# 68 dense expert tiles instead of 72 in a hybrid mLSTM, S5 and PEER block: fewer dense tiles, more gather steps, other buffer counts

## The chip, the core and the metric

The kernel runs on one core of a Trainium2 chip. TensorE multiplies matrices, VectorE (DVE in the profile) and ScalarE (ACT) work element by element, GpSimd (POOL) issues indirect DMAs (gathers by a list of row numbers), and SyncE (SP) issues ordinary DMAs. The metric is the device time of one execution in microseconds; it is compared as the median of several runs. The profiles come from single executions.

## The reference

The input is 512 tokens of 2048 features in float32. One layer is computed: a norm, an input projection, an mLSTM mixer beside an S5 state-space mixer, an output projection with a residual sum, and then the PEER part, which is what the change touches:

```
q   = rmsnorm(h) @ wq                        # 8 heads, two halves of 128
s   = q . subkeys                            # 128 scores for each half
idx = top 16 of (top 16 of s1 + top 16 of s2)    # expert number = i1 * 128 + i2
gate = softmax(top scores)
act = gelu(x . u_tab[idx])                   # 128 (token, expert) pairs per token
h  += sum over pairs of gate * act * v_tab[idx]
out = rmsnorm(h) * final_g
```

There are 128 x 128 = 16384 experts, each with a row of 2048 numbers in `u_tab` and one in `v_tab`. Each of the 512 tokens picks 128 experts, so there are 65536 pairs.

## The kernel before

Gathering two rows for each of the 65536 pairs would be slow, so the kernel treats most experts densely. `NT` tiles of 128 experts are multiplied with all 512 tokens, whether a token picked them or not, and a gate matrix that is zero for the pairs not picked removes the rest. `NF` of these tiles are fixed (the first experts by number); `NSEL` more are lists of the experts picked most often, counted at run time by `select`. Pairs whose expert is in no dense tile are rare pairs. They are handled by gather steps: the tokens are sorted by their number of rare pairs and cut into four blocks of 128; for block b there are `SB[b]` steps on the `u` side and as many on the `v` side, and one step gathers one row of 2048 numbers for each of up to 128 tokens. If a token has more rare pairs than its block has steps (a whole block's worth for the later blocks), `flag` is set and `rare_rest` does what is left behind the V pass, one gather after the other.

All matrix products are made of three passes (`mm3`, lines 114 to 117) over operands split in a high and a low part.

The PEER part has these stages:

- **The U pass** (lines 1555 to 1575) goes through `NT` x 4 units, a quarter tile each. `u_load` brings a tile of 128 expert rows into `ur` (from SP for the fixed tiles, by a gather from GpSimd for the others), two tiles ahead. `u_unit` transposes four blocks on TensorE into PSUM (`tu`), and ScalarE copies the high part `uh`; `u_low` makes the low part `ul` on VectorE; `h_unit` multiplies. After the fourth quarter ScalarE takes the GELU into `hg`, and SP stores it (lines 1503 to 1505). `h_step` keeps transposes three units and low parts two units ahead of the products.
- **Beside it** the same loop hands out side work. Each unit adds a budget (2.9 until the lists are ready, then `UBUD`), and each piece of side work gives back its own cost when it yields. First come the end of the routing, `select`, and `flags`. Then (from unit `n0` on) two jobs share the budget: `gbuild`, 64 pieces at 3.45 that build the gate matrix in eight chunks of 64 tokens, and `rare`, gather steps at 2.5 each. `gbuild` has a due time (`GEND`); when it is ahead of it, gather steps run.
- **A chunk of `gbuild`** makes one-hot operands `go` on VectorE, multiplies 24 small matrices per piece on TensorE, and ScalarE copies the result into `Gb`, of which there is one. Then SP stores 4 MB from it into `gt_d` with four DMAs whose pieces are 256 bytes long (line 1456), and `UT["hold"]` keeps `gbuild` from its next piece for some units.
- **The V pass** (lines 1642 to 1662) goes through `NT` tiles twice, once for each half of the 2048 output columns. A unit loads half a tile of `v` (`vr`), the stored activations (`hgl`) and in half 0 the gate tile (`gt`), multiplies the gate in (`v_gate`, and stores the product in `w_d` for half 1), splits both operands and runs 24 matmuls. The gather steps that the U pass has not done are spread evenly over the units, except the last `VEND`.

A gather step is `row_gather` into a `gr` tile (issued on GpSimd) and one VectorE instruction: `mac_u` (line 1343) or `mac_v` (line 1350). `rare` issues gathers ahead: 2 deep in the U pass, 4 deep in the V pass, where `gr_tile` takes its tiles from two pools of two each.

```
        bud += UBUD if n0 is not None else 2.9
...
            gb_next = n0 is None or n >= UT["hold"] and UT["gb_n"] * (GEND - n0) <= (n - n0) * (T // 8)
            c = pump1("a") if gb_next else 0
            c = c or (pump1("g") if n0 is not None else 0)
```

Of the kernel before, what the change touches and what calls it, by code (L numbers as in the profile page):

```python
# [8 lines left out]
F32 = mybir.dt.float32  # L9
F32R = mybir.dt.float32r  # L10
I32 = mybir.dt.int32
U32 = mybir.dt.uint32
BF16 = mybir.dt.bfloat16
AF = mybir.ActivationFunctionType
OP = mybir.AluOpType
# [4 lines left out]
P = 128  # L20
T = 512
D = 2048
# [3 lines left out]
NEG = -1.0e30  # L26
BIGNEG = -3.0e38
MAGIC = 12582912.0
NF = 28
NSEL = 44  # L30
NT = NF + NSEL
JN = P - NF
CLIP = 32
RW = 64
SB = (54, 36, 31, 26)
JUNK = F32
UBUD = 2.8
GEND = 262
VPRE = 276
VEND = 14  # L40


# [5 lines left out]
def hybrid_block(ctx: ExitStack, tc: tile.TileContext, x, norm1_g, w_in, b_gates, conv_w, mnorm_g,  # L48
# [3 lines left out]
    v, s, g, pe, sp = nc.vector, nc.scalar, nc.gpsimd, nc.tensor, nc.sync  # L52
# [3 lines left out]
    def pool(name, bufs, side="left"):  # L56
        return tc.tile_pool(name=name, bufs=bufs, side=side, reuse_waits="tile")
# [37 lines left out]
    with pool(name="tmp", bufs=1, side="right") as tmp:  # L95
# [8 lines left out]
        p = tp_bank([P, 96])  # L104
# [749 lines left out]
    front.close()  # L854

    pk = ctx.enter_context(pool(name="pk", bufs=1, side="right"))
    subT = pk.tile([P, 2, P], F32, name="subT")
    iotaF = pk.tile([P, P], F32, name="iotaF")
    pcol = pk.tile([P, 1], F32, name="pcol")
    jt = pk.tile([P, P, 2], BF16, name="jt")  # L860
# [4 lines left out]
    DT = pk.tile([P, 5, T], BF16, name="DT")  # L865
# [2 lines left out]
    esel2 = pk.tile([P, 2, NSEL], I32, name="esel2")  # L868
    rl = pk.tile([P, TB, 2 * RW + 1], I32, name="rl")
    flag = pk.tile([P, 1], I32, name="flag")  # L870

    xn_d = dram.tile([T, D], F32, name="xn_d")
    gt_d = dram.tile([P * P, T], F32, name="gt_d")
# [43 lines left out]
    with pool(name="n2", bufs=1) as n2:  # L917
# [18 lines left out]
        p = tp_bank([P, 2, P])  # L936
# [6 lines left out]
        v.tensor_copy(jt, iotaF[:, :, None].to_broadcast([P, P, 2]))  # L943
        v.tensor_scalar(tri, iotaF, pcol, None, op0=OP.is_gt)
    mix.close()
    ixs = ExitStack()
    ix = ixs.enter_context(pool(name="ix", bufs=1, side="right"))
    i1T, i2T, gT = (ix.tile([P, T], F32, name=n) for n in ("i1T", "i2T", "gT"))
    tks = ExitStack()
    tk = tks.enter_context(pool(name="tk", bufs=1, side="right"))  # L950
    gate = tk.tile([P, TB, P], F32, name="gate")
# [79 lines left out]
    for h in range(8):  # L1031
# [7 lines left out]
        for a in range(2):  # L1039
            p = tp_bank([P, TB, P])  # L1040
# [7 lines left out]
    UT = {}  # L1048
# [23 lines left out]
    def spread(row, n):  # L1072
        r = row.rearrange("p (a b) -> p a b", b=2)
        return r[:, :, None, :].to_broadcast([P, r.shape[1], n, 2])

    def select():
# [11 lines left out]
        for c2 in range(0, T + 64, 32):  # L1088
            if c2 < T:
                oa = ck.tile([P, 16, JN, 2], BF16, name="oa", bufs=2)  # L1090
                ob = ck.tile([P, 16, P, 2], BF16, name="ob", bufs=2)
                onehot(oa, NF, JN, i1b, c2, 32)
                onehot(ob, 0, P, i2b, c2, 32)
# [7 lines left out]
        c = ck.tile([P, JN], F32, name="c")  # L1101
        v.tensor_scalar(c, cnt, float(CLIP), None, op0=OP.min)
        oha = ck.tile([P, JN, P], BF16, name="oha")
# [9 lines left out]
        p = tp_bank([P, CLIP])  # L1113
# [4 lines left out]
        k = ck.tile([P, 2, CLIP], F32, name="k")  # L1118
# [25 lines left out]
        v.memset(sf, 1.0)  # L1144
        sel = sf[:, NF:]
        v.scalar_tensor_tensor(sel, ex, need, eq, op0=OP.is_lt, op1=OP.mult)
# [9 lines left out]
        ab = ck.tile([P, 2, JN], F32, name="ab")  # L1156
        v.tensor_copy(ab, sli[:, 1:3])
        yield
        ohv = ck.tile([P, JN, 2, NSEL], BF16, name="ohv")
        for j in range(0, JN, 20):  # L1160
            js = slice(j, j + 20)
            v.tensor_tensor(oha[:, js], ab[:, 1, js, None].to_broadcast([P, 20, P]),
                            iotaF[:, None, :].to_broadcast([P, 20, P]), op=OP.is_equal)
            yield
            v.tensor_tensor(ohv[:, js, 1], ab[:, 0, js, None].to_broadcast([P, 20, NSEL]),
                            iotaF[:, None, 1:NSEL + 1].to_broadcast([P, 20, NSEL]), op=OP.is_equal)
            v.tensor_tensor(ohv[:, js, 0], ohv[:, js, 1],
                            iotaF[:, NF + j:NF + j + 20, None].to_broadcast([P, 20, NSEL]), op=OP.mult)
            v.tensor_scalar(ohv[:, js, 1], ohv[:, js, 1], pcol, None, op0=OP.mult)
            yield  # L1170
        p = tp_bank([P, 2, NSEL])
# [151 lines left out]

    def gr_tile():
        UT["n"] = UT.get("n", -1) + 1
        pl = UT["rp2"] if "rp2" in UT and UT["n"] % 4 > 1 else UT["rp"]
        t = pl.tile([P, D], F32, name="gr", bufs=2)
        key = "r2" if "rp2" in UT and pl is UT["rp2"] else "r1"
        UT[key] = UT.get(key, 0) + 1
        if UT[key] <= 2:  # L1330
            v.memset(t, 0.0)
        return t

# [24 lines left out]

    rjobs = [(w, b, j) for w in range(2) for b in range(TB) for j in range(SB[b])]

    def rare():
        q = []
        k = 0
        xa = nx = None
        for n, (w, b, j) in enumerate(rjobs):
            if n == 0 or nx is None and n + 6 < len(rjobs) and rjobs[n + 6][2] == 0 and "rp2" in UT:
                nx = xa_tile()
                gather(nx, h1_d if rjobs[min(n + 6, len(rjobs) - 1)][0] and n else xn_d, tokc(rjobs[n + 6][1] if n else b))
            if j == 0:
                if nx is None:  # L1370
                    nx = xa_tile()
                    gather(nx, h1_d if w else xn_d, tokc(b))
                xa, nx = nx, None
            while k < len(rjobs) and k < n + (4 if "rp2" in UT else 2):
                t = gr_tile()
                row_gather(t, rjobs[k][0], rl[:, rjobs[k][1], rjobs[k][2]:rjobs[k][2] + 1])
                q.append(t)
                k += 1
            t = q.pop(0)
            a = racts[:, b, j:j + 1]  # L1380
            if w:
                mac_v(t, a, xa)
            else:
                mac_u(t, xa, a)
            if j == SB[b] - 1:
                if w:
                    rare_out(b, xa)
                else:
                    rare_w(b, 0, SB[b], racts[:, b, 0:SB[b]])
            UT["rare_n"] = n + 1  # L1390
            yield 2.5
# [31 lines left out]
    def gbuild():  # L1423
        stk = ExitStack()
        gb = stk.enter_context(pool(name="gb", bufs=1, side="right"))
        GC = 64
        GN = 8

        def fill(Gb, o, t0):
            for t4 in range(0, GN, 4):  # L1430
                p = tp_bank([P, 4, P])
                for t in range(4):
                    a, c = divmod(t4 + t, 2)
                    for k in range(3):
                        pe.matmul(p[:, t, :], o[1][:, a, :, c], o[2 + k][:, a, :, c], start=k == 0, stop=k == 2)
                s.activation(Gb[:, :, t0 + t4:t0 + t4 + 4], p.rearrange("p t i -> p i t"), AF.Copy)

        gv = gt_d.rearrange("(i k) t -> k i t", k=P)
        todo = []
        for c in range(0, T, GC):  # L1440
            Gb = gb.tile([P, P, GC], F32, name="Gb")
            for t0 in range(c, c + GC, GN):
                o = [gb.tile([P, GN // 2, P, 2], BF16, name=f"go{i}", bufs=2) for i in range(5)]
                onehot(o[0], 0, P, i1b, t0, GN)
                onehot(o[1], 0, P, i2b, t0, GN)
                for k in range(3):
                    v.tensor_tensor(o[2 + k], o[0], spread(DT[:, 2 + k, t0:t0 + GN], P), op=OP.mult)
                todo.append((Gb, o, t0 - c))
                UT["gb_n"] += 1
                yield 3.45  # L1450
                if len(todo) > 1:
                    fill(*todo.pop(0))
            while todo:
                fill(*todo.pop(0))
            for a in range(0, P, 32):
                sp.dma_start(gv[:, a:a + 32, c:c + GC], Gb[:, a:a + 32, :])
            UT["hold"] = UT["step"] + 4
        stk.close()
        yield 0.1

    ustk = ExitStack()
    up = ustk.enter_context(pool(name="up", bufs=1))

    def u_load(i):
        ur = up.tile([P, D], F32, name="ur", bufs=2)
        if i < NF:
            sp.dma_start(ur, u2[i * P:(i + 1) * P, :])
        else:
            assert UT["sel"]
            gather(ur, u2, esel[:, i - NF:i - NF + 1])  # L1470
        UT["r", i] = ur
# [16 lines left out]

    def u_low(i, q):
        uh, p = UT.pop(("p", i, q))  # L1490
        ul = up.tile([P, 4, P], F32R, name="ul", bufs=4)
        v.tensor_tensor(ul, p, uh.bitcast(F32), op=OP.subtract)  # L1492
        UT["u", i, q] = (uh, ul)

    def h_unit(i, q):
        if q == 0:
            UT["h", i] = mm_bank()
        uh, ul = UT.pop(("u", i, q))
        for a in range(4):
            k = q * 4 + a  # L1500
            mm3(UT["h", i], uh[:, a, :], ul[:, a, :], xh[:, k, :], xl[:, k, :], k == 0, k == 15)
        if q == 3:
            hg = up.tile([P, T], F32, name="hg", bufs=2)
            s.activation(hg, UT.pop(("h", i)), AF.Gelu)
            sp.dma_start(hg_d[i], hg)

# [48 lines left out]
    for n, (i, q) in enumerate(units):  # L1555
# [8 lines left out]
        while bud > 0:  # L1564
# [5 lines left out]
            c = pump1("a") if gb_next else 0  # L1570
            c = c or (pump1("g") if n0 is not None else 0)
# [69 lines left out]
    o = banks()  # L1641
    for n, (h, i) in enumerate(vunits):
        if n == NT:
            for k, b_ in enumerate(o):
                s.activation(F0[:, k // 2, (k % 2) * 512:(k % 2) * 512 + 512], b_, AF.Copy)
            o = banks()
# [21 lines left out]
    with tc.If(fl_v > 0):  # L1668
        rare_rest(fb)
        for tb in range(TB):  # L1670
            t = fb.tile([P, D], F32, name="rg")
# [44 lines left out]
```

## Time and profile before

| | |
|---|---|
| median of 3 runs | 3192.2 us (3181.93 to 3195.36) |
| the profiled execution | 3185.52 us, span 3183.6 us |
| mean granted TensorE clock in it | 0.962 |
| TensorE busy | 2926.7 us, 92% |
| VectorE busy | 2226.3 us, 70% |
| ScalarE busy | 978.8 us, 31% |
| GpSimd busy | 848.9 us, 27% |
| moved by DMA | 691.92 MB, mean 217 GB/s |

The shares are means over stages that differ: the DMA engines are busy for three to four tenths of the first third and almost wholly in the last third. A busy TensorE is not one at its peak, since matmuls overlap and their ends are modelled. The granted clock is given as a share of full speed, 2.4 GHz; its other level is 1.2 GHz.

### The profile page before, as it was taken

To read this page: it belongs to the slowest core of one execution; us is meant where nothing else is said; L and a number is where in the kernel's file an instruction comes from. 1 tells how busy PE (TensorE), PEld (TensorE's weight loads), DVE (VectorE), ACT (ScalarE), POOL (GpSimd) and SP (SyncE) were. 2 spreads that over 40 slices of the span, in tenths; PEclk is the share of its full clock that TensorE was granted. 3 is DMA by queue.
4 is the path that set the end of the run, shared out by engine and by line. 5 is a ranking of instruction groups with operands and counts; after the bars stand their busy time and mean duration, and the time that the engine had idled before them with its cause. 6 is when DMAs were issued, how large, how long until landed. Compare 5 with 4: busy or idle time off the path is not lost. (4 is left out here: it accounts for less than half of the span.)

```text
span 3183.6 us, 44978 instructions
## 1 busy us (share of the span) xinstructions
PE 2926.7 (92%) x17540; PEld 2462.5 (77%) x17540; DVE 2226.3 (70%) x3665; ACT 978.8 (31%) x1491; POOL 848.9 (27%) x656
## 2 busy tenths in 40 slices
PE   7999999999799999998999998896698888899997
PEld 5888978899688887886777787775477666688886
DVE  7467544432388977874767876774688888889885
ACT  5343555432322321121222222221122222232223
POOL 3000111000200000001222222222244888647860
PEclk9999999999899999997999999998899999999999
DMA  4422444353322221634778667779899997999983
GB/s 142 129 87 85 102 108 119 105 175 133 134 87 86 100 95 67 242 140 147 258 241 283 181 193 241 252 245 323 296 395 381 403 401 240 407 408 406 394 328 134
DMA packets 366140, 691.92 MB, mean 217 GB/s; under 512 B 169490, under 2 KB 248850, under 8 KB 320338
## 3 DMA queue, kind: packets, MB, share of 16 engines
q0 software_dynamic: 74240, 393.57, 33.0%
q1 hardware_dynamic: 291680, 295.40, 28.2%
q8 instruction: 140, 2.29, 0.3%
q14 instruction: 80, 0.66, 0.1%
HBM read 644.04 MB, written 96.86 MB: 233 GB/s over the span
## 5 line engine op out<-in xcount | busy, mean ns | idle before, releaser
L115 PE MATMUL mm<-xh,uh 128*128 128x512 f32 x1152 | 494.6, 429 | 0.0
L117 PE MATMUL mm<-xh,ul 128*128 128x512 f32 x1152 | 465.1, 404 | 7.5 <-DVE ul L1492 7.5
L116 PE MATMUL mm<-xl,uh 128*128 128x512 f32 x1152 | 465.3, 404 | 0.0
L1343 DVE SCALAR_TENSOR_TENSOR junk<-gr,xa 128x2048 f32<-128x2048 f32 x147 | 335.8, 2284 | 163.0 <-DMA gr<-in_peer_u_dram,rl 149.0
L1350 DVE SCALAR_TENSOR_TENSOR xa<-gr,racts,xa 128x2048 f32<-128x2048 f32 x147 | 345.4, 2350 | 58.1 <-DMA gr<-in_peer_v_dram,rl 56.8
L112 DVE TENSOR_TENSOR wl<-wr,wh 128x1024 fp32r<-128x1024 f32 (+1 forms) x144 | 187.1, 1302 | 240.2 <-ACT wh L111 240.1
L1484 ACT ACTIVATE uh<-tu 128x512 fp32r<-128x512 f32 x288 | 171.6, 600 | 501.4 <-PE tu L1482 489.4
L1346 POOL DMA_INDIRECT gr<-in_peer_u_dram,rl x147 | 180.2, 1226 | 460.8 <-DVE junk L1343 419.1
L115 PE MATMUL mm<-wh,xh 128*128 128x256 f32 (+1 forms) x1024 | 294.6, 288 | 0.0
L117 PE MATMUL mm<-wh,xl 128*128 128x256 f32 (+1 forms) x1024 | 288.8, 282 | 1.8 <-DVE xl L112 1.8
L116 PE MATMUL mm<-wl,xh 128*128 128x256 f32 (+1 forms) x1024 | 289.0, 282 | 0.0
L116 PE MATMUL tp<-vl,ewh 128*128 128x512 f32 x576 | 232.5, 404 | 61.1 <-DVE vl L112 61.0
L1346 POOL DMA_INDIRECT gr<-in_peer_v_dram,rl x147 | 248.6, 1691 | 131.9 <-DVE xa L1350 83.3
L117 PEld LDWEIGHTS mm<-xh,ul 128*128 128x128 f32 x1152 | 225.7, 196 | 62.4 <-DVE ul L1492 8.7
L117 PE MATMUL mm<-xh,wl 128*128 128x512 f32 x640 | 255.9, 400 | 12.1 <-DVE wl L112 12.1
L111 ACT ACTIVATE ewh<-hgl 128x512 fp32r<-128x512 f32 x144 | 91.0, 632 | 561.4 <-DVE hgl L1546 275.9
L115 PE MATMUL mm<-xh,wh 128*128 128x512 f32 x640 | 258.3, 404 | 0.0
L116 PEld LDWEIGHTS mm<-xl,uh 128*128 128x128 f32 x1152 | 227.5, 197 | 39.6
L115 PEld LDWEIGHTS mm<-xh,uh 128*128 128x128 f32 x1152 | 227.1, 197 | 39.4
L116 PE MATMUL mm<-xl,wh 128*128 128x512 f32 x640 | 254.9, 398 | 0.0
L1482 PE MATMUL tu<-ident,ur 128*128 128x128 f32 x1152 | 182.1, 282 | 73.0 <-DVE ul L1492 72.3
L111 ACT ACTIVATE wh<-wr 128x1024 fp32r<-128x1024 f32 (+1 forms) x144 | 166.8, 1161 | 260.5 <-PE mm L117 103.0
(498 smaller groups left out, 6080.4 us busy)
## 6 DMA issues: line engine op xcount, KB each, us to landing
wr<-in_w_in_dram SPq DMA_DIRECT2D x80, 512.0 KB, 3.6
gt_d<-Gb SPq DMA_DIRECT2D x32, 1024.0 KB, 17.0
ur<-in_peer_u_dram SPq DMA_DIRECT2D x28, 1024.0 KB, 5.0
vr<-in_peer_v_dram SPq DMA_DIRECT2D x56, 512.0 KB, 14.9
hg_d<-hg SPq DMA_DIRECT2D x72, 256.0 KB, 2.2
hgl<-hg_d SPq DMA_DIRECT2D x72, 256.0 KB, 9.3
w_d<-hgl SPq DMA_DIRECT2D x72, 256.0 KB, 7.6
hgl<-w_d SPq DMA_DIRECT2D x72, 256.0 KB, 7.9
```

Source lines behind the costliest of these rows:

```text
L111: s.activation(hi, src, AF.Copy)
L112: v.tensor_tensor(lo, src, hi.bitcast(F32), op=OP.subtract)
L115: pe.matmul(o, ah, bh, start=start, stop=False)
L116: pe.matmul(o, ah, bl, start=False, stop=False)
L117: pe.matmul(o, al, bh, start=False, stop=stop)
L1343: v.scalar_tensor_tensor(UT["junk"], t, 1.0, xg, op0=OP.mult, op1=OP.mult, accum_out=a)
L1346: g.indirect_dma_start(out=t, out_offset=None, in_=v2 if w else u2, in_offset=IOA(ap=col, axis=0), bounds_check=P * P - 1, oob_is_err=False)
L1350: v.scalar_tensor_tensor(acc, t, a, acc, op0=OP.mult, op1=OP.add)
L1482: pe.transpose(p[:, a, :], ur[:, k * P:(k + 1) * P], ident)
L1484: s.activation(uh, p, AF.Copy)
```

## The change

- `NF` goes from 28 to 22 and `NSEL` from 44 to 46: 68 dense tiles instead of 72. `GEND` and `VPRE`, 262 and 276 before, are now written as `4 * NT - 26` and `4 * NT - 12`, which is 246 and 260.
- `SB` goes from (54, 36, 31, 26) to (57, 39, 34, 29): 159 gather steps on each side instead of 147.
- `UBUD` goes from 2.8 to 3.0, and the pause of `gbuild` after each store from 4 units to 8 (`HOLD`).
- Buffers: `ur` 3 instead of 2; `gr` 3 in the first pool (2 in the second as before), so gathers run 3 deep in the U pass and 5 deep in the V pass. In exchange `ul` has 3 instead of 4, `hg` 1 instead of 2, and the `go` operands are 4 tiles instead of 5: the third product is written over the one-hot it is made from. `subT` and the index tiles move to a pool of their own, allocated earlier.
- `select` allows a last chunk shorter than 20 columns, since 128 - 22 = 106 is no multiple of 20.

```
-NF = 28
-NSEL = 44
+NF = 22
+NSEL = 46
-SB = (54, 36, 31, 26)
+SB = (57, 39, 34, 29)
-UBUD = 2.8
-GEND = 262
-VPRE = 276
+UBUD = 3.0
+HOLD = 8
+GEND = 4 * NT - 26
+VPRE = 4 * NT - 12
...
     def gr_tile():
         UT["n"] = UT.get("n", -1) + 1
-        pl = UT["rp2"] if "rp2" in UT and UT["n"] % 4 > 1 else UT["rp"]
-        t = pl.tile([P, D], F32, name="gr", bufs=2)
-        key = "r2" if "rp2" in UT and pl is UT["rp2"] else "r1"
-        UT[key] = UT.get(key, 0) + 1
-        if UT[key] <= 2:
+        key = "rp2" if "rp2" in UT and UT["n"] % 5 > 2 else "rp"
+        nb = {"rp": 3, "rp2": 2}[key]
+        t = UT[key].tile([P, D], F32, name="gr", bufs=nb)
+        UT["c" + key] = UT.get("c" + key, 0) + 1
+        if UT["c" + key] <= nb:
             v.memset(t, 0.0)
         return t
...
-            while k < len(rjobs) and k < n + (4 if "rp2" in UT else 2):
+            while k < len(rjobs) and k < n + (5 if "rp2" in UT else 3):
...
-                        pe.matmul(p[:, t, :], o[1][:, a, :, c], o[2 + k][:, a, :, c], start=k == 0, stop=k == 2)
+                        pe.matmul(p[:, t, :], o[1][:, a, :, c], o[2 + k if k < 2 else 0][:, a, :, c], start=k == 0, stop=k == 2)
...
-                o = [gb.tile([P, GN // 2, P, 2], BF16, name=f"go{i}", bufs=2) for i in range(5)]
+                o = [gb.tile([P, GN // 2, P, 2], BF16, name=f"go{i}", bufs=2) for i in range(4)]
...
-                    v.tensor_tensor(o[2 + k], o[0], spread(DT[:, 2 + k, t0:t0 + GN], P), op=OP.mult)
+                    v.tensor_tensor(o[2 + k if k < 2 else 0], o[0], spread(DT[:, 2 + k, t0:t0 + GN], P), op=OP.mult)
...
-            UT["hold"] = UT["step"] + 4
+            UT["hold"] = UT["step"] + HOLD
...
-        ur = up.tile([P, D], F32, name="ur", bufs=2)
+        ur = up.tile([P, D], F32, name="ur", bufs=3)
...
-        ul = up.tile([P, 4, P], F32R, name="ul", bufs=4)
+        ul = up.tile([P, 4, P], F32R, name="ul", bufs=3)
...
-            hg = up.tile([P, T], F32, name="hg", bufs=2)
+            hg = up.tile([P, T], F32, name="hg")
```

## Rows read from the trace of the kernel before

**Rows 1.** Stretches: length, busy PE, PEld, DVE, ACT, POOL; clock, DMA, GB/s.

```profile
1044.00:1471.00 427.00, 422.14 (x3392) 351.13 (x3393) 327.85 (x706) 97.49 (x175) 5.14 (x19) 0.96 0.34 125
1471.00:2135.00 664.00, 602.58 (x3960) 501.67 (x3959) 479.25 (x643) 179.57 (x319) 157.74 (x130) 0.95 0.72 237
2135.00:2281.00 146.00, 101.61 (x461) 79.60 (x459) 81.99 (x87) 19.69 (x35) 35.71 (x34) 0.85 0.84 292
2281.00:2440.00 159.00, 134.49 (x555) 106.94 (x556) 134.49 (x141) 40.26 (x51) 63.09 (x36) 0.94 0.97 375
2440.00:2755.00 315.00, 272.82 (x1131) 215.53 (x1131) 259.20 (x208) 76.80 (x97) 261.91 (x155) 0.97 0.94 361
2755.00:3084.00 329.00, 325.28 (x1424) 268.77 (x1423) 300.44 (x206) 99.76 (x127) 211.26 (x120) 0.99 0.98 394
```

**Rows 2.** Timeline in the U pass: start, length, what ran.

```profile
1606.63 0.60 PE L1482 MATMUL tu<-ident,ur 128*128 128x128 f32 x4
...
1609.84 0.60 PE L1482 MATMUL tu<-ident,ur 128*128 128x128 f32 x4
...
1613.05 1.55 PE L1435 MATMUL tp<-go,go 128*128 128x128 bf16 x24
...
1614.44 0.61 PE L1482 MATMUL tu<-ident,ur 128*128 128x128 f32 x4
```

**Rows 3.** Waits, 1471 to 2135 us: in total, times, longest.

```profile
POOL ur L1051 <- PE tu L1482: 227.2, 35, 19.6
...
ACT Gb L1436 <- DMA gt_d<-Gb: 100.0, 7, 27.0
...
DVE junk L1343 <- DMA gr<-in_peer_u_dram,rl: 87.4, 17, 11.6
...
PE tu L1482 <- DVE ul L1492: 35.5, 13, 10.2
PE tp L1435 <- ACT Gb L1436: 25.9, 4, 9.9
```

**Rows 4.** Groups by line, 1471 to 2135, then 2135 to 2281 us.

```profile
L1343 DVE SCALAR_TENSOR_TENSOR junk<-gr,xa 128x2048 f32<-128x2048 f32 x85 | 194.0, 2283 | 92.7 <-DMA gr<-in_peer_u_dram,rl 87.4 <-DMA xa<-xn_d,rl 5.1
...
L1343 DVE SCALAR_TENSOR_TENSOR junk<-gr,xa 128x2048 f32<-128x2048 f32 x28 | 64.1, 2289 | 62.0 <-DMA gr<-in_peer_u_dram,rl 53.6 <-DMA xa<-xn_d,rl 8.3
```

**Rows 5.** Timeline of SP's queue around the second gate store.

```profile
1656.30 19.17 SPq L1456 DMA_DIRECT2D gt_d<-Gb  x4
1675.56 15.39 SPq L1505 DMA_DIRECT2D hg_d<-hg  x3
```

**Rows 6.** Timeline of ScalarE at the same time, the GELUs.

```profile
1658.88 0.60 ACT L1504 ACTIVATE hg<-mm 128x512 f32<-128x512 f32 x1 [2.12 <-PE mm L117]
...
1671.69 0.60 ACT L1504 ACTIVATE hg<-mm 128x512 f32<-128x512 f32 x1 [2.17 <-PE mm L117]
```

**Rows 7.** The tile `hg`: issue to landing of its 72 stores.

```profile
DMA to landing us min/median/max: 2.0/2.2/14.6
```

**Rows 8.** Groups by line, 2440 to 2755 us (half 0, gathered tiles).

```profile
L1350 DVE SCALAR_TENSOR_TENSOR xa<-gr,racts,xa 128x2048 f32<-128x2048 f32 x62 | 145.9, 2353 | 37.7 <-DMA gr<-in_peer_v_dram,rl 37.2
L1346 POOL DMA_INDIRECT gr<-in_peer_v_dram,rl x65 | 105.3, 1620 | 27.3 <-issue 15.5 <-DVE xa L1350 4.4 <-DVE junk L1343 3.4
L1051 POOL DMA_INDIRECT vr<-in_peer_v_dram,esel x44 | 83.6, 1901 | 13.4 <-issue 10.1 <-DMA vr<-in_peer_v_dram,esel 0.9 <-ACT vh L111 0.9
...
L1051 POOL DMA_INDIRECT gt<-gt_d,esel x44 | 70.1, 1593 | 13.4 <-issue 12.8 <-DMA vr<-in_peer_v_dram,esel 0.3 <-DMA w_d<-hgl 0.3
L112 DVE TENSOR_TENSOR vl<-vr,vh 128x1024 fp32r<-128x1024 f32 x47 | 57.7, 1228 | 0.1
...
L1546 DVE TENSOR_TENSOR hgl<-hgl,gt 128x512 f32<-128x512 f32 x47 | 32.2, 686 | 16.8 <-DMA gt<-gt_d,esel 14.9 <-issue 1.8
```

**Rows 9.** Groups by line, 2755 to 3084 us (half 1).

```profile
L1350 DVE SCALAR_TENSOR_TENSOR xa<-gr,racts,xa 128x2048 f32<-128x2048 f32 x84 | 197.2, 2348 | 20.3 <-DMA gr<-in_peer_v_dram,rl 19.6
...
L112 DVE TENSOR_TENSOR vl<-vr,vh 128x1024 fp32r<-128x1024 f32 x61 | 74.4, 1219 | 7.2 <-ACT vh L111 6.9
```

More of the change, by code (lines that the diff above doesn't have):

```diff
@@ L856, in hybrid_block @@
     pk = ctx.enter_context(pool(name="pk", bufs=1, side="right"))
-    subT = pk.tile([P, 2, P], F32, name="subT")
     iotaF = pk.tile([P, P], F32, name="iotaF")
@@ L870, in hybrid_block @@
     flag = pk.tile([P, 1], I32, name="flag")
+    ixs = ExitStack()
+    ix = ixs.enter_context(pool(name="ix", bufs=1, side="right"))
+    i1T, i2T, gT = (ix.tile([P, T], F32, name=n) for n in ("i1T", "i2T", "gT"))
+    subT = ix.tile([P, 2, P], F32, name="subT")
     xn_d = dram.tile([T, D], F32, name="xn_d")
@@ L945, in hybrid_block @@
     mix.close()
-    ixs = ExitStack()
-    ix = ixs.enter_context(pool(name="ix", bufs=1, side="right"))
-    i1T, i2T, gT = (ix.tile([P, T], F32, name=n) for n in ("i1T", "i2T", "gT"))
     tks = ExitStack()
@@ L1160, in select @@
         for j in range(0, JN, 20):
-            js = slice(j, j + 20)
-            v.tensor_tensor(oha[:, js], ab[:, 1, js, None].to_broadcast([P, 20, P]),
-                            iotaF[:, None, :].to_broadcast([P, 20, P]), op=OP.is_equal)
+            m = min(20, JN - j)
+            js = slice(j, j + m)
+            v.tensor_tensor(oha[:, js], ab[:, 1, js, None].to_broadcast([P, m, P]),
+                            iotaF[:, None, :].to_broadcast([P, m, P]), op=OP.is_equal)
             yield
-            v.tensor_tensor(ohv[:, js, 1], ab[:, 0, js, None].to_broadcast([P, 20, NSEL]),
-                            iotaF[:, None, 1:NSEL + 1].to_broadcast([P, 20, NSEL]), op=OP.is_equal)
+            v.tensor_tensor(ohv[:, js, 1], ab[:, 0, js, None].to_broadcast([P, m, NSEL]),
+                            iotaF[:, None, 1:NSEL + 1].to_broadcast([P, m, NSEL]), op=OP.is_equal)
             v.tensor_tensor(ohv[:, js, 0], ohv[:, js, 1],
-                            iotaF[:, NF + j:NF + j + 20, None].to_broadcast([P, 20, NSEL]), op=OP.mult)
+                            iotaF[:, NF + j:NF + j + m, None].to_broadcast([P, m, NSEL]), op=OP.mult)
             v.tensor_scalar(ohv[:, js, 1], ohv[:, js, 1], pcol, None, op0=OP.mult)
```

## The prediction

> **What bounds the kernel now.** Read the table of stretches first [rows 1]. The change acts behind 1044 us: the U pass (1044 to 2281), which forms the hidden activations of 72 expert tiles, and the V pass (from 2281 to near the end), which goes over the same tiles twice, 144 units. In the U pass TensorE is busy, except at its end (101.61 of 146 us). In the V pass look at three columns together: while half 0 runs on gathered tiles (2440 to 2755) GpSimd is busy 261.91 of 315 us, the DMA engines 0.94 and VectorE 259.20; in half 1 TensorE has 325.28 of 329 us, with DMA at 0.98 and VectorE at 300.44. So the U pass has holes to be filled, the V pass has nearly none.
>
> The timeline gives the unit of account [rows 2]: from one set of four transposes to the next is 3.21 us, a quarter tile, which I call a step; one with a block of 24 gate matmuls in it takes 4.60, so a block costs 1.4 to 1.55 us. Then the waits of the middle stretch [rows 3]: GpSimd stands 227.2 us for a `ur` buffer, and row gathers queue behind it; ScalarE stands 100.0 us for the one `Gb` buffer, of which 25.9 reach TensorE; VectorE stands 87.4 us for gathered rows, of which 35.5 reach TensorE.
>
> **Steps and gather counts.** The side loop is arithmetic. Before: 288 steps; the preliminaries end at step 107; (288-107)x2.8 = 507 units of budget, 64 gate blocks take 64x3.45 = 221, the other 286 pay 115 gather steps at 2.5. The trace has 85+28 = 113 in the two stretches, which bears it out [rows 4]. After: select has six chunks where it had five, 5 units more, two steps at 2.9: the preliminaries end at 109. (272-109)x3.0 = 489, less 221, pays 108. So the U pass does fewer of a longer list, and the V pass gets 318-108 = 210 where it had 294-115 = 179, in 122 units (136-14) where it had 130: 1.72 a unit, not 1.38.
>
> **U pass, before the gate blocks.** 427 us for 107 steps [rows 1]: two steps more, at 4.0, are **+8 us**. The lists of experts are ready at step 70 and first wanted at 80, where the fixed tiles now end, so nothing waits there.
>
> **U pass, middle (steps 109 to 246, was 107 to 262).** Before: 155 steps x 3.21 + 64x1.55 = 597 of 664 us, so 67 us are stalls and a lower clock (0.95). After: 137 steps make 539. Then, one by one:
> - The start (list load, first gather) is the same in both: 13 us, estimated from the 10.2 us of the longest wait behind it and what follows.
> - The `Gb` stall: with a pause of 8 steps in place of 4 the first fill comes some 3.5 steps, 12 us, later; the seven waits average 14.3 us [rows 3], the longest 27. What is left reaches TensorE with some 4 us, not 25.9.
> - `hg` loses its second buffer. SP issues four gate stores in 19.17 us [rows 5], and the `hg` store stands behind them in the same queue: the GELU of 1658.88 [rows 6] is stored from 1675.56 on, and lands after up to 14.6 us [rows 7]. The next GELU, at 1671.69, doesn't wait now; with one buffer it would, some 16 us. Eight such bursts at 1 to 18 us make about 90 us of ScalarE waiting, as much as `Gb` had, and by the same exchange (25.9 for 100.0) 25 us of TensorE. Bounds 0 and 40. So this wait takes the place of the one removed.
> - Gathers: the third `ur` buffer takes the 227.2 us off GpSimd's queue. But with a pause of 8 steps the whole share of gathers of a chunk (17 steps x 3.0 less 27.6, that is 9.4) falls into the pause, 1.2 per step. Two buffers give one gather per 5.0 us at the pass's end (below), three one per 3.4: six and a half behind three that lie ready need about 29 us, the pause has 25.7. With up to 6 us of slack in the three-step lead that is 0 to 5 us each; I take 3, together 25 us for 8. Here `ul` going from 4 to 3 buffers counts too: VectorE may start a split only when the matmuls of three steps ago are done, so the slack is shorter by some 2 us.
> - Lower clock behind the stalls: 15 us of the 24 that 810 us less work and stalls leave.
>
> Sum 539+13+4+25+25+15 = 621, **-43 us**; ends 567 (no gather or `hg` stall) and 665.
>
> The gate operand written in place of the one-hot has as many instructions as before, on the same engines; it costs nothing. `subT` and the index tiles only change their place in memory, and `GEND` and `VPRE` stand as far from the end of the pass as before.
>
> **U pass, end (26 steps).** 28 gather steps in 146 us [rows 4], where the steps need 83: 5.2 us each, VectorE 62.0 us idle for them, with two buffers. A turnaround is thus about 10 us, and three buffers give one per 3.4 us. The larger budget wants 31: 105 us, or 125 if the turnaround grows to 12 under more traffic, or 90 if it all hides. I take 113: **-33 us**.
>
> **V pass.** Eight units less, 31 gather steps more. Per unit VectorE has 1.23 for `vl`, 0.69 for the gate product in half 0 and as much for the split of the same shape, and 2.35 per gather step [rows 8]: 2.61 + 1.72x2.35 = 6.65 in half 0 where it had 5.85, 5.96 in half 1 where it had 5.15; neighbours overlap by about 0.08 us each, which leaves 6.3 and 5.7. GpSimd per gathered unit: 1.90+1.59+1.72x1.62 = 6.3 and 0.3 of issue for each, 7.4; the row of before gives 315/47 = 6.7 us per unit. I take 7.0 for the 22 fixed units of half 0 (was 159/25 = 6.4), 7.3 for the 46 gathered, 5.8 for 54 units of half 1 (was 329/61 = 5.4 [rows 9]) and 5.4 for the last 14: 154+336+313+76 = 879. Before: 28x6.4+44x6.7+72x5.4 = 863. **+16 us.** Ends: all added work hidden, 140+308+367 = 815, -48; everything at the busiest engine plus the idling of today (7.3, 7.6, 6.1), 916, +53. The fifth gather buffer speaks for the middle.
>
> **Sum.** 8-43-33+16 = -52 on the profiled execution's own 3185.5 us (3183.6 of span): 3133. The runs shown have a median of 3192.2, 0.2% above that execution: 3140 by it. I say **3138**.
>
> **Rivals.**
> *The V pass goes by bandwidth (ends slower).* The three V stretches moved 375x159+361x315+394x329 = 303 MB in 803 us, 377 GB/s [rows 1]. 31 steps bring at most 31x1.05 MB (128 rows of 8 KB), the lost units take 8 away: 327 MB. At 377 that is 867 us, +64, and the whole 3185+8-43-33+64 = 3181: no change. At 361, the lowest of the three stretches, it is 906, +103, and 3220: slower. It decides once V loses more than 68 us. For it: DMA at 0.94 to 0.98 in all three. Against it: half 1 ran at 394, and the 361 stood beside a GpSimd that was full. Chance 0.10, half of it slower.
> The Trainium skill's page "DMA: Bandwidth & Descriptors", section "Specifications", puts a core's share of HBM at about 358 GB/s; by that 327 MB are 913 us and the whole ends near 3227. The trace's 394 over 329 us speaks against that number, so it raises no chance here.
> *The stalls only change place.* `hg` at its upper end (40) and the gathers in the pauses (40) keep the middle at 651, -13, and the end of the pass at 125: 3185+8-13-21+16 = 3175. For it: the 16 us worked out above. Against: a third buffer in front of both. Chance 0.10, mostly no change.
> *Everything hides.* Middle 567, end 90, V -5 with five gathers in flight: 3185+8-97-56-5 = 3035; something of it, 3060 to 3090, chance 0.16.
> *The overflow path runs.* By the reference's inputs the fullest token has 57 rare pairs, and the new first limit is 57: no room. Over it, 97 more gather steps on each side run one behind the other, at 10 us some 1.9 ms. Chance 0.02.
> *Forecast,* 3090 to 3176: chance 0.62.
>
> **Numbers.** A measurement of this kernel tells about 0.5%, 16 us, from no change: faster is below 3176, slower above 3208. Faster 0.62+0.16+0.03 = 0.81; no change 0.07+0.05 = 0.12; slower 0.05+0.02 = 0.07. The range for 8 in 10 leaves out half of "everything hides", the slow bandwidth case and the overflow: **3075 to 3188**.
>
> **What would show it.** Right: the wait of GpSimd for `ur` gone; `Gb` waits under 30 us in all; a new wait of ScalarE's GELU (L1504's line) for the `hg` store, 50 to 120 us; 107 or 108 gathers of `u` in the U pass; the stretch behind the last gate block near 113 us; half 0 at 7.0 to 7.4 us per unit. Wrong: half 1 above 6.1 us a unit, which would be bandwidth; no GELU wait; gathers that turn around in more than 13 us, so that three buffers give no more than two did; or a U pass that shortens by no more than its 16 steps (51 us).

## The result and the profile after

The changed kernel takes 3234.25 us in the median (3231.27 to 3240.61, four runs), the kernel before 3187.06 us (3181.49 to 3195.36): a ratio of 1.0151, 95% interval 1.0135 to 1.0167. It is slower by 1.5%, where 3138 us were forecast and 3188 was the upper end of the range. The profiled execution took 3232.3 us, with a span of 3230.4.

Cut both spans at four points: the first and the last copy into `Gb`, the last GELU of the U pass, and the last `mac_v`. The tile views of the changed kernel give the first and the last start of each:

```profile
L1439 ACT ACTIVATE Gb<-tp x128: 592/598/653, 1520.8 to 2153.7; 128x512 f32<-128x512 f32 x128
...
L1507 ACT ACTIVATE hg<-mm x68: 590/598/605, 1059.3 to 2275.5; 128x512 f32<-128x512 f32 x68
...
L1353 DVE SCALAR_TENSOR_TENSOR xa<-gr,racts,xa x159: 2337/2351/2408, 2512.2 to 3139.8; 128x2048 f32<-128x2048 f32 x159
```

The same views of the kernel before say 1508.5 and 2143.0, 2280.3, and 3084.4. In microseconds:

| stretch | before | after | difference | forecast |
|---|---|---|---|---|
| to the first copy into `Gb` | 1508.5 | 1520.8 | +12.3 | +8 |
| first to last copy into `Gb` | 634.5 | 632.9 | -1.6 | -43 |
| to the last GELU of the U pass | 137.3 | 121.8 | -15.5 | -33 |
| V pass to its last gather step | 804.1 | 864.3 | +60.2 | +16, together with the row below |
| the rest | 99.2 | 90.6 | -8.6 | |

The U pass has 16 steps less, 51 us of TensorE work, and is 5 us shorter. The V pass has eight units less and is 52 us longer. The forecasts of both passes failed, and in separate places. Three stretches of the changed kernel (columns as in [rows 1]) show what the passes are like now:

```profile
1488.00:2154.00 666.00, 549.98 (x3743) 458.29 (x3743) 466.65 (x620) 168.64 (x301) 153.81 (x120) 0.92 0.66 219
...
2440.00:2780.00 340.00, 267.67 (x1068) 207.24 (x1066) 284.94 (x230) 74.06 (x92) 288.91 (x168) 0.94 0.93 357
2780.00:3140.00 360.00, 326.38 (x1369) 256.63 (x1369) 326.17 (x213) 98.04 (x124) 241.40 (x137) 0.99 0.98 391
```

In the first line TensorE, the first figure behind the length, is busy for 550 of 666 us, where it had 603 of 664 [rows 1]: 53 us of work less, and 55 us of idling more. In the last, half 1 of the V pass, it idles for 34 of 360 us, where it idled for 4 of 329.

The waits of the changed kernel, 1488 to 2154 us (in total, times, longest):

```profile
POOL ur L1053 <- PE tu L1485: 175.8, 10, 30.6
ACT hg L1507 <- DMA hg_d<-hg: 163.6, 6, 29.5
...
DVE ul L1495 <- ACT uh L1487: 89.9, 6, 16.8
PE tu L1485 <- DVE ul L1495: 86.5, 16, 16.5
...
DVE junk L1346 <- DMA gr<-in_peer_u_dram,rl: 53.3, 22, 9.8
...
PE tp L1438 <- ACT Gb L1439: 29.5, 2, 15.6
```

Against [rows 3] ScalarE's wait for the store of `Gb` has gone from the list, and one that was not there stands in its place: its GELU waits 25 to 30 us at a time for the store of the one `hg`. While it waits, the copies behind it are late, VectorE's splits are late for that (the third line), and TensorE idles 86.5 us for splits where it idled 35.5. With the 29.5 us at the gate matmuls (the last line) that is all of its 116 us of idling. The wait for late gather rows fell from 87.4 to 53.3 us, the way the third `gr` buffer was to move it; no run takes that buffer away by itself. GpSimd's wait for `ur` is still 175.8 us, in ten waits instead of 35, where the forecast had it gone.

Why the `hg` store is so late shows in SP's queue and in ScalarE's timeline at the second gate store of the changed kernel. SP first:

```profile
1658.63 31.50 SPq L1459 DMA_DIRECT2D gt_d<-Gb  x4
1690.23 17.02 SPq L1508 DMA_DIRECT2D hg_d<-hg  x2
```

and ScalarE:

```profile
1667.68 0.60 ACT L1507 ACTIVATE hg<-mm 128x512 f32<-128x512 f32 x1 [2.23 <-PE mm L118]
...
1706.30 0.60 ACT L1507 ACTIVATE hg<-mm 128x512 f32<-128x512 f32 x1 [26.22 <-DMA hg_d<-hg]
```

The GELU of 1667.68 is stored from 1690.23 on, because SP takes 31.5 us to issue the four gate stores. Before, it took 19.2 [rows 5]. Over the eight chunks the issue took 16.5 to 29.5 us before, 21.1 in the mean, and takes 15.9 to 43.1 now, 32.8 in the mean. That length is the first thing that the forecast took as given and that changed.

### The profile page after: what moved, and what is told of

The parts are those of the page before. It is cut to its first block, busy times and chain, and to the rows that moved or that the text cites. A ratio compares the mean times of both kernels' runs of the same rounds, so it can differ in the third digit from the quotient of the medians.

```text
span 3230.4 us, 44225 instructions
## 1 busy us (share of the span) xinstructions
PE 2854.2 (88%) x17098; PEld 2385.8 (74%) x17098; DVE 2269.3 (70%) x3670; ACT 955.9 (30%) x1455; POOL 946.3 (29%) x688
## 5 line engine op out<-in xcount | busy, mean ns | idle before, releaser
L116 PE MATMUL mm<-xh,uh 128*128 128x512 f32 x1088 | 465.6, 428 | 0.0
L118 PE MATMUL mm<-xh,ul 128*128 128x512 f32 x1088 | 437.8, 402 | 0.8 <-DVE ul L1495 0.8
L117 PE MATMUL mm<-xl,uh 128*128 128x512 f32 x1088 | 438.0, 403 | 0.0
L1346 DVE SCALAR_TENSOR_TENSOR junk<-gr,xa 128x2048 f32<-128x2048 f32 x159 | 363.3, 2285 | 90.2 <-DMA gr<-in_peer_u_dram,rl 81.9
L1353 DVE SCALAR_TENSOR_TENSOR xa<-gr,racts,xa 128x2048 f32<-128x2048 f32 x159 | 373.5, 2349 | 52.2 <-DMA gr<-in_peer_v_dram,rl 50.2
L1349 POOL DMA_INDIRECT gr<-in_peer_u_dram,rl x159 | 236.9, 1490 | 469.1 <-DVE junk L1346 367.1
L1349 POOL DMA_INDIRECT gr<-in_peer_v_dram,rl x159 | 266.0, 1673 | 120.0 <-DVE xa L1353 67.4
L1495 DVE TENSOR_TENSOR ul<-tu,uh 128x512 fp32r<-128x512 f32 x272 | 185.2, 683 | 150.2 <-ACT uh L1487 115.7
L118 PEld LDWEIGHTS mm<-xh,ul 128*128 128x128 f32 x1088 | 212.2, 195 | 51.8 <-DVE ul L1495 1.2
L1485 PEld LDWEIGHTS tu<-ident,ur 128*128 128x128 f32 x1088 | 129.5, 144 | 154.0 <-DVE ul L1495 129.5
```

Source lines behind the costliest of these rows:

```text
L116: pe.matmul(o, ah, bh, start=start, stop=False)
L117: pe.matmul(o, ah, bl, start=False, stop=False)
L118: pe.matmul(o, al, bh, start=False, stop=stop)
L1346: v.scalar_tensor_tensor(UT["junk"], t, 1.0, xg, op0=OP.mult, op1=OP.mult, accum_out=a)
L1349: g.indirect_dma_start(out=t, out_offset=None, in_=v2 if w else u2, in_offset=IOA(ap=col, axis=0), bounds_check=P * P - 1, oob_is_err=False)
L1353: v.scalar_tensor_tensor(acc, t, a, acc, op0=OP.mult, op1=OP.add)
```

## The experiments

**The second `hg` buffer back.** Theory A: this wait is the loss. Theory B: something else holds the pass up, and the wait only covers it. The 2 KB come from `select`, where three small tiles are written over ones that are done with, and two constants move to the pool of the index tiles.

```
-            hg = up.tile([P, T], F32, name="hg")
+            hg = up.tile([P, T], F32, name="hg", bufs=2)
```

> The changed kernel with the second hg buffer back (2 KB found by writing three small tiles of select over ones that are done with). Theory A, the GELU that waits for the store of the one hg buffer is what keeps the U pass from getting shorter: its waits of 26 to 32 us at the gate stores go, and with them most of the 112 us that TensorE idles behind them; the U pass ends 90 to 130 us sooner, the V pass stays at about 905 us, and the whole is 3105 to 3140 us. Theory B, the dense gathers in the eight-step pause and the long gate store hold the pass up anyway, and the GELU's wait only covers it: ScalarE's wait moves to Gb or the idling to late gathers, and the whole is 3190 us or more.

Measured: 3208.32 us, ratio to the kernel before 1.0045 (1.0025 to 1.0065). That is 26 us of the 90 to 130 that theory A wanted. The waits of this kernel, 1488 to 2130 us:

```profile
ACT Gb L1439 <- DMA gt_d<-Gb: 93.5, 5, 21.7
...
PE tp L1438 <- ACT Gb L1439: 65.5, 6, 14.7
```

With a second `hg` the wait for `Gb` is back, 17 to 22 us each time, in spite of the longer pause, and 65.5 us of it reach TensorE. Two waits for the `hg` store stay as well, of 17 and 31 us. So theory A holds for a fifth to under a third of what it claimed, and the whole is above the 3190 us that theory B named.

**One `hg` buffer in the kernel before.**

```
-            hg = up.tile([P, T], F32, name="hg", bufs=2)
+            hg = up.tile([P, T], F32, name="hg")
```

> The kernel before with one hg buffer in place of two and nothing else changed. Theory A: the GELU behind each gate store waits; with four-step pauses and SP's store bursts of 19 us the waits are 10 to 20 us each, part of them in the shadow of the Gb waits, and the whole grows by 30 to 70 us. Theory B: within 15 us of the kernel before.

Measured: 3194.91 us, ratio 1.0010 (0.9994 to 1.0026). So the missing buffer by itself is not the loss: with stores as short as they were in the kernel before, the one buffer costs nothing that can be told from zero. Three GELU waits of 19 to 21 us appeared and `Gb` waited less.

**The counts alone, and everything but the counts.** The first takes only `NF`, `NSEL`, `SB` and the due times of the change into the kernel before; the second is the changed kernel with two `hg` buffers and the old counts.

```
-NF = 28
-NSEL = 44
+NF = 22
+NSEL = 46
-SB = (54, 36, 31, 26)
+SB = (57, 39, 34, 29)
```

> The kernel before with the counts of the change alone (22 fixed and 46 listed tiles, 159 steps, the due times that go with them) and the buffers, the pause and the budget of before. The budget of 2.8 pays only 95 gather steps in the U pass, so the V pass gets 223, 1.83 a unit. If the V pass pays for gather steps at the rate seen (47 us for 31 steps and 8 units less), it gets 60 to 70 us longer, the U pass 55 us shorter, and the whole is within 20 us of the kernel before: the trade of tiles for gathers is worth nothing by itself. If the V pass was slowed by the five gathers in flight and not by their number, the whole is 3130 us or less.

> The changed kernel with the second hg buffer back and the old counts (28 and 44 tiles, 147 steps): buffers, pause and budget of the change without its trade. 129 gather steps fall into the U pass and 165 into the V pass, 1.27 a unit. If the trade of tiles for gathers is worth nothing, it is as fast as the changed kernel with two hg buffers or faster: 3080 to 3120 us. If the trade is a gain of its own that the hg wait hid, it is 40 us or more slower than that.

Measured: the counts alone 3250.5 us, ratio 1.0189 (1.0168 to 1.0210); the rest without them 3180.26 us, 0.9968 (0.9955 to 0.9980). Against the changed kernel with two `hg` buffers the old counts are 28 us faster. So the trade of tiles for gathers, put at no loss, is a loss of 28 us with the buffers, pause and budget of the change and of 61 with those of before, and what goes with the trade is worth 9 us where 70 and more were expected. The counts alone did end the U pass 45 us sooner (55 expected), but the V pass to its last gather step took 924.1 us, 120 more than before, where 60 to 70 were expected: it has 226 gather steps to do, not 181.

**No gathers beside the store.** Theory C: the store is long because the pause fills with gather steps. The only edit to the kernel with two `hg` buffers is that no gather step is handed out in the pause. The budget of these units is dropped, so the U pass does 47 gather steps and not 108.

```
-            c = c or (pump1("g") if n0 is not None else 0)
+            c = c or (pump1("g") if n0 is not None and n >= UT["hold"] else 0)
```

> The changed kernel with two hg buffers, and no gather step in the eight steps of the pause: 47 gather steps fall into the U pass in place of 108, the other 61 into the V pass. Theory C, the gate store itself gets long because the pause fills with gathers: SP's issue of the four stores takes 31 to 43 us with 7 or 8 gathers beside it and falls below 20 us here, the waits of 17 to 22 us for Gb and of the GELU for hg fall to under 5 us, and the stretch from the first gate block to the last gets 50 to 90 us shorter than its 608 us. Theory D, the store is long by its 256-byte pieces whatever runs beside it: issue and waits stay within a quarter of what they were. The V pass gets 271 gather steps in either case and is not the question.

Measured: 3229.72 us in one execution. SP's queue at the third gate store, with two `hg` buffers and the crowded pause:

```profile
1738.85 41.00 SPq L1459 DMA_DIRECT2D gt_d<-Gb  x4
```

and with the quiet one:

```profile
1703.77 17.71 SPq L1459 DMA_DIRECT2D gt_d<-Gb  x4
```

41.00 us with seven row gathers and three gathers of expert tiles (`ur`) issued during it, 17.71 with no row gather and one of an expert tile. All eight stores took 14.3 to 18.9 us, where they took 16.0 to 48.2. No wait for the `Gb` store or for the `hg` store is left in the U pass, and the stretch from the first copy into `Gb` to the last is 511.0 us, 98 less. The stretch with two `hg` buffers and the crowded pause, then with the quiet one:

```profile
1488.00:2130.00 642.00, 550.74 (x3743) 459.64 (x3742) 466.63 (x620) 169.29 (x302) 151.70 (x120) 0.93 0.69 227
```

```profile
1488.00:2031.00 543.00, 531.06 (x3735) 446.60 (x3734) 351.13 (x511) 169.97 (x298) 74.50 (x65) 0.99 0.65 196
```

Theory C stands, D falls: the issue is not long whatever runs beside it. The 98 us are not the store's alone, since 61 gather steps left the stretch as well. The traces split them roughly: TensorE's idling fell from 91 us to 12, its busy time from 551 to 531 at a granted clock of 0.99 in place of 0.93, and of the 91 us of idling 65.5 stood at `Gb` and 25.5 at late splits. The other side is in the same run: the V pass takes the 61 gather steps and reaches its last one 1011 us behind the end of the U pass, not 866, which is 2.4 us for each. In the U pass each of them had cost 2.0 (its end came 123 us sooner), so the whole is 21 us slower than with the crowded pause.

**The pause at four steps.**

```
-HOLD = 8
+HOLD = 4
```

> The changed kernel with two hg buffers and the pause at 4 steps as before. Theory C: fewer gathers beside the store, so a shorter store, but ScalarE comes back to Gb some 12 us sooner; the two nearly cancel, Gb waits of 10 to 20 us stay, and the whole is within 15 us of the 3208 us with eight steps. Theory D: the store is as long as with eight steps and the waits grow by the 12 us each, some 60 us of TensorE in all: 3250 us or more.

Measured: 3210.28 us, ratio 1.0062 (1.0043 to 1.0081), 2 us from the eight steps. SP's issue came down to 27 to 30 us at six of the eight stores and ScalarE came back sooner, which nearly cancels, as theory C had it. The `Gb` waits came out longer than expected, six of 21.7 us in the mean. Between four and eight steps the length of the pause does nothing here.

**Bytes or VectorE in the V pass.** Two kernels take away one of the two loads that a gather step puts on the V pass.

```
+        o, tab = (t[:, :512], v2.rearrange("e (h c) -> (e h) c", h=4)) if w else (t, u2)
...
+        q4 = acc.rearrange("p (h c) -> p h c", h=4)
+        v.scalar_tensor_tensor(q4, t[:, None, :512].to_broadcast([P, 4, 512]), a, q4, op0=OP.mult, op1=OP.add)
```

> The changed kernel, but the gathers of the v side bring 512 of the 2048 columns (2 KB a row in place of 8 KB), and the VectorE instruction of the step reads these 512 four times: as many instructions, elements and descriptors as before, a quarter of the bytes. The result is not the reference's. If the V pass is slowed by DMA bandwidth, half 1 falls from 6.19 us a unit to 5.7 or less, which is what VectorE takes. If by VectorE's instructions, or by GpSimd's queue with its number of descriptors, it stays above 6.0.

```
-        v.scalar_tensor_tensor(acc, t, a, acc, op0=OP.mult, op1=OP.add)
+        v.scalar_tensor_tensor(acc[:, :1024], t[:, :1024], a, acc[:, :1024], op0=OP.mult, op1=OP.add)
```

> The changed kernel, but the VectorE instruction of a v gather step works on 1024 of the 2048 columns, so it costs half, with all bytes gathered as before. The result is not the reference's. If VectorE's time sets the V pass, half 1 falls from 6.19 us a unit to TensorE's 5.43. If bandwidth sets it, half 1 stays at 5.9 or above.

Each ran once (3226.16 and 3213.96 us); what is compared is a stretch of half 1 with 55 units in it (55 instructions that split `vl` in each). The changed kernel, then the narrow gathers, then the half instruction:

```profile
2780.00:3130.00 350.00, 317.04 (x1329) 249.39 (x1330) 316.21 (x206) 94.27 (x119) 237.65 (x135) 0.99 0.99 396
```

```profile
2805.00:3125.00 320.00, 307.93 (x1319) 247.15 (x1318) 312.68 (x204) 93.05 (x117) 249.44 (x135) 0.99 0.70 220
```

```profile
2770.00:3115.00 345.00, 312.38 (x1318) 246.80 (x1317) 215.58 (x205) 92.24 (x117) 152.85 (x134) 0.99 1.00 399
```

Read the length, the third busy time (VectorE), and the last two columns. A quarter of the bytes: 320 us, and VectorE is busy for 313 of them. Half the VectorE work: 345 us, with VectorE at 216 and the DMA engines full at 399 GB/s. So bandwidth sets half 1, at 6.3 to 6.4 us a unit, and VectorE stands right behind it at 5.8, a little above the 5.7 that was expected of it. The Trainium skill's page "DMA: Bandwidth & Descriptors", section "Specifications", gives a core some 358 GB/s of HBM; the 396 GB/s over 350 us and the 399 over 345 say that this core got more, so here the ceiling lies higher than that number.

Half 0 behaves otherwise. There the narrow gathers gained nothing: from ScalarE's copy of the first unit's `vh` to that of the first unit of half 1 it took 7.44 us a unit, 7.21 in the changed kernel, while the half instruction brought 6.90. GpSimd's groups, 2450 to 2770 us, in the changed kernel:

```profile
L1053 POOL DMA_INDIRECT gt<-gt_d,esel x42 | 93.4, 2223 | 12.8 <-issue 12.5 <-DMA gt<-gt_d,esel 0.3
...
L1053 POOL DMA_INDIRECT vr<-in_peer_v_dram,esel x43 | 75.0, 1745 | 13.1 <-issue 12.8 <-DMA gt<-gt_d,esel 0.3
```

and with the half instruction:

```profile
L1053 POOL DMA_INDIRECT gt<-gt_d,esel x43 | 66.5, 1547 | 20.8 <-DMA gr<-in_peer_v_dram,rl 11.3 <-issue 8.8 <-DMA gt<-gt_d,esel 0.3
L1053 POOL DMA_INDIRECT vr<-in_peer_v_dram,esel x43 | 55.0, 1280 | 15.8 <-issue 15.2 <-DMA gt<-gt_d,esel 0.3 <-DMA vr<-in_peer_v_dram,esel 0.3
```

In the changed kernel GpSimd waits for hardly anything there but its own issue, and its gathers of `gt` and `vr` got shorter (2223 to 1547 ns, 1745 to 1280) when VectorE had less to do. Its row gathers did not (1397 and 1499 ns in the same stretches). That GpSimd's queue sets the gathered part of half 0 is argued from these rows and not shown; no run gave it less to issue. The Trainium skill's page "GPSIMD Engine Reference", section "Specifications", says that GpSimd shares its SBUF interfaces with VectorE and that instructions of VectorE with two SBUF inputs contend for them. The `gt` and `vr` rows agree with that, the row gathers do not, and the rows can't tell it from other ways in which less VectorE work might help.

**The gathers spread.** If the crowd is what makes the store long, the same gather steps can be handed out better: in the pause one in every second unit, what is left of the budget behind it, one or two pieces a unit.

```
+        if n0 is not None and n < UT["hold"]:
+            if n % 2 == 0:
+                bud -= pump1("g")
+            continue
+        left = bud if n0 is None else 2.4 if n % 2 else 4.5
+        while bud > 0 and left > 0:
...
+            gb_next = n0 is None or UT["gb_n"] * (GEND - n0) <= (n - n0) * (T // 8)
...
+            left -= c
```

All have two `hg` buffers. The first keeps the 68 tiles, the second has 72 and the old steps, the third 72 and the old budget (`UBUD = 2.8`).

> The changed kernel with two hg buffers, its 68 tiles and 159 steps, and the side work handed out otherwise: in the eight steps of the pause one gather step in every second unit, the rest of the budget is kept and spent behind the pause, one or two pieces a unit. 106 gather steps fall into the U pass, as before (108). Theory C, the store is long because gathers crowd beside it: SP's issue of the four stores comes down to 20 to 28 us, most of the Gb waits of 17 to 22 us go, the U pass ends 30 to 70 us sooner than with the crowded pause, and the whole is 3140 to 3180 us. Rival, a gather step costs the U pass 2 us wherever it stands: within 15 us of 3208 us.

> The same handing out with the old counts (72 tiles, 147 steps) and the budget of 3.0: 128 gather steps in the U pass, 166 in the V pass, 1.28 a unit. The V pass stays at its 841 us of the run with old counts. Theory C: the U pass gets 30 to 70 us shorter than its end at 2293 us there, the whole 3110 to 3150 us. Rival: within 15 us of 3180 us. If trading tiles for gathers costs 30 us by itself, this stands some 30 us below the same handing out with 68 tiles.

> The same with a budget of 2.8: 115 gather steps in the U pass, 179 in the V pass. If a gather step costs 2 us in either pass, within 15 us of the run with 3.0. If the U pass takes more of them for nothing once they are spread, 15 to 30 us slower than that, by the V pass.

Measured: 3198.09 us, ratio 1.0032 (1.0018 to 1.0047); 3155.1 us, 0.9902 (0.9884 to 0.9920); 3130.28 us, 0.9824 (0.9800 to 0.9848). The spreading gained 10 us with 68 tiles, where the rival's forecast came true (within 15 us of 3208) and theory C's did not, and 25 with 72, outside both. It didn't shorten the store: SP's issue took 34 us in the mean of the eight with 68 tiles (35 without spreading) and 28 with 72 (28), though with 68 tiles only 37 row gathers were issued during the eight stores and not 59. So that gathers lengthen the store is shown by the quiet pause, but not how many it takes, nor that spreading cures it. The same hand-out with 72 tiles is 43 us faster than with 68. The third beats both kernels, by 1.8% the one before. It is 25 us below the second, outside both of its expectations: 13 gather steps fewer end its U pass 34 us sooner, and its V pass takes them for 12 us (from the last GELU to the last `mac_v`: 795.2 and 783.3). So with 72 tiles a gather step cost 2.6 us in the U pass, spread as they were, and 0.9 in the V pass.

**A pause of ten steps in the best one.**

```
-HOLD = 8
+HOLD = 10
```

> 72 tiles, two hg buffers, budget 2.8, one gather step in every second unit of the pause, and the pause 10 steps long in place of 8. If what is left of the Gb waits (7 to 13 us at six stores) is what still holds the U pass up, they fall below 6 us and the whole is 5 to 25 us below 3130 us. If VectorE and TensorE are full behind the pause, where the pieces are now closer together, the U pass gets as much longer there: 3125 to 3145 us.

Measured: 3151.97 us, ratio 0.9869 (0.9849 to 0.9890), 22 us slower than with eight and outside both expectations. Three waits for the `hg` store, of 14 to 16 us, came back, and four for `Gb` stayed. SP's issue of the gate stores took 32.4 us in the mean, 25.1 with eight steps. Eight was the better length; what made the stores longer with ten is open.

## Why the prediction was wrong

*What held.* The gather counts (107 gathers issued before the last GELU of the U pass, forecast 108); the two extra steps of the preliminaries (+12 us, forecast +8); less waiting of VectorE for gathered rows; and that the GELU would wait for the one `hg` where `Gb` waited before. Half 0 of the V pass took 490.5 us by ScalarE's copies, forecast 490, but that is partly luck: the kernel before took 465.3 us by the same measure, where the forecast reckoned with 474, so half 0 grew by 25 us and not by 16.

*The step that failed in the U pass: "with a pause of 8 steps in place of 4 the first fill comes some 3.5 steps, 12 us, later ... what is left reaches TensorE with some 4 us".* It subtracted the longer pause from the waits of before, and so took the store for as long as it was. But the prediction's own paragraph on gathers had worked out that the whole share of a chunk's gathers, 9.4, now falls into the pause. The two were never put together: those gathers run beside the store, which is 4 MB in pieces of 256 bytes, and SP's issue of it grew from 21.1 to 32.8 us in the mean (43.1 at the first). The `hg` wait, put at about 90 us of ScalarE and 25 of TensorE, was taken from a burst of 19 us too; it came to 195.8 us of ScalarE in seven waits of 25 to 32 us, and TensorE's idling in the middle stretch grew by 55 us, where the sum left room for 15 more of stalls and lower clock together. With the second `hg` back the same long store showed at `Gb`: what this step had put at 4 us of TensorE measured 65.5. So the middle got 1.6 us shorter, not 43. With two `hg` buffers and no gathers in the pause it took 511 us, 98 less than with two and a crowded pause, which counts the store and the 61 gather steps that left the U pass together. The Trainium skill's page "DMA: Bandwidth & Descriptors", section "Queues, rings and completion order", says that each DMA engine takes turns between the queues that have work, one packet at a time. The 17.7 and 41.0 us, without and with row gathers of 8 KB rows beside the store, agree with it; nothing here looked at the packets themselves.

*The step that failed in the V pass: "5.8 for 54 units of half 1 ... and 5.4 for the last 14".* The price came from VectorE's busy time, and where the bytes were taken away it nearly held (5.8). In the changed kernel it was the rival's mechanism that decided: half 1 was at 394 GB/s before, and a unit of it that also carries 1.72 gather steps needs 6.3 to 6.4 us at 396. Half 1 took 415 us by ScalarE's copies where 389 were forecast; before, it had taken 393. Of the 52 us that the V pass got longer, half 1 has 21.5, half 0 25, and the way into the pass 5; the forecast was 0 for half 1 and 16 for half 0. The rival had the place wrong too, since it let bandwidth set all of the V pass: half 0 got no faster with a quarter of the bytes. What made half 0 grow by 9 us more than forecast is open.

*Smaller errors of the working.* The ends of the middle's range, 567 and 665, come to 571 and some 660 when its own terms are added up. And the 35.5 us of TensorE were put down to late gather rows, while in the same view VectorE's splits also wait 39.8 us for ScalarE's copies; how much of the 35.5 came from rows is not known.

*What follows for the trade.* In the V pass a unit less saves little, because the gather steps that stood beside it stay. With 68 and 72 tiles handed out alike (the two spread kernels with a budget of 3.0), the stretch between the copies into `Gb` is 51 us shorter with 68 (587.3 and 637.9), and the V pass up to its last gather 80 us longer (863.4 and 783.3), with 213 gather steps done behind the U pass and not 168. The U pass that was cut was also the place that took gather steps.

*The end of the U pass* got 15.5 us shorter where 33 were forecast: one of the seven waits for `hg`, of 32 us, falls into it. Whether the fourth `ul` buffer, given up for room, costs anything by itself was not tried.

## What to carry to other kernels

A pause made for a transfer must be looked at for what runs in it: work that brings its own transfers can make the transfer last longer than the pause (here 41 us of issue in a pause of eight steps, some 26 us), and what stands behind it in its queue waits with it. Whether the store's small pieces make it the one that suffers was not tried. Before dense work is traded for gathers, ask what limits the stretch that takes the gathers with the dense work gone: where that is bandwidth, a tile less saves only its bytes, not its matmuls.

## What the runs showed of the hardware

The issue of one and the same 4 MB store took SP 17.7 us with one gather of an expert tile beside it and 41.0 us with three of these and seven row gathers. With half of a VectorE instruction taken away, two kinds of gather issue on GpSimd went from 1745 to 1280 ns and from 2223 to 1547, a third from 1397 to 1499. And the granted clock of TensorE over the U pass's gate stretch was 0.93 of 2.4 GHz with 91 us of idling in 642 us, and 0.99 with 12 in 543.
